# Bringing Branch B's inverse rms to the channel rows: a DRAM scratch row instead of TensorE transposes

## The chip, the core and the metric

The kernel runs on one core of a Trainium2 chip. The time is device microseconds of one execution; before the change the median of three runs is 1976.4 us (1971.2 to 1978.23). A core has a matrix engine, TensorE (PE; its weight loads are shown apart as PEld), a vector engine (DVE), an activation engine (ACT), a general engine (POOL) and a queue engine (SP), on which every DMA of this kernel is issued. Each engine takes its instructions strictly in order. Matrix results land in PSUM, a small memory of banks of 128 × 512 fp32 values; everything else lies in SBUF, 128 partitions wide.

## The reference

One encoder layer is applied to two independent requests ("groups"), each 1024 tokens × 1024 channels, with shared weights. Cut to what matters:

```
h    = rms_norm(x, norm_g) * (1 + scale) + shift
qa, ka, va, za, qb, kb, vb, zb, ga, gb = split(h @ w_in)
oa   = gqa_attention(rope(rms(qa)), rope(rms(ka)), va) * silu(za)      # 8 heads of 64
ob   = softmax(q0 k0) @ v - lam * softmax(q1 k1) @ v                   # 4 heads of 128
ob   = rms_norm(ob, subln_g) * (1 - lam_init)                          # over a head's 128 channels
ob   = ob * silu(zb)
merged = sigmoid(ga) * (oa @ w_proj_a) + sigmoid(gb) * (ob @ w_proj_b)
y    = x + gate * (merged @ w_out)
```

The change concerns the fourth and fifth lines of Branch B: each token of each head is divided by the rms of its 128 values.

## The kernel before

All of it is fp32 made from pairs of a rounded high part and a low rest, so a product takes three matmuls; scores and the values of a head are kept with channels on the partitions and tokens along the row. The two groups run one after the other. A group has these parts:

- the input projection, woven with attention: `qa_gen`, `qkb_gen`, `vb_gen` (matmuls at L514), and the gate paths z, ga, gb by `z_gen` (matmuls at L703), whose results are put to DRAM at L712 as `zd`;
- `attention`: 32 units of Branch A, then 16 units of Branch B (four heads, each four pairs of query tiles). A unit has scores (L734, L735), a softmax (L736 to L738), `flip` (a vector transpose at L771 and four DMA copies at L776, `q<-p`), and the values (L796, L797 for A, L836 for B in `b_values`). Attention's instructions get a higher priority than the work woven around them;
- at the end of a Branch B unit the squares of the output are summed over channels by a matmul with a column of ones (L858), so that the sum has the tokens on the partitions, and copied to `ssB` (L860), [128 tokens, head, 8 tiles]. After a head's last unit POOL turns the 8 columns into inverse rms values (L863 to L866);
- `gated_gen`: for each half of the tokens (`hf`) and each block of 128 channels e (0 to 3 are Branch A, 4 to 7 the heads of Branch B), the attention output `od` and gate `zd` are loaded, the gate gets its SiLU (L931), both are multiplied, and the row is multiplied by its per-token factor `rb`, which must now lie along the row and be the same on every partition (L946). Then the high part (L947, ACT) and low part (L948, DVE) are written for the projection;
- `merge_gen` for Branch A and then Branch B: 16 products of 12 matmuls each (L976), each multiplied by a sigmoid gate that is loaded at L966; the gate's sigmoid is at L967, the product with A's result at L987, with B's at L982;
- `out_gen`: the output projection (L1005).

For Branch A the factor comes through DRAM: the 64 rows of inverse sums are transposed once, stored as `rA` (L918), and each tile loads its row to 64 partitions at a time into a tile of the tag `tab` (L935), two buffers deep. The same two buffers hold the tables cosA and sinA earlier in a group. For Branch B the factor comes by TensorE: each column of 128 tokens is broadcast to 128 columns and transposed with the identity, four times for the 512 tokens of a tile (L941), into a PSUM bank, and L946 reads it there. There are 2 groups × 4 heads × 2 halves = 16 such tiles, so 64 transposes.

PSUM: three banks of the tag `f`, and two double banks `s` for scores. `gbank()` gives an `f` bank, or, where no attention runs (`alone`), the first half of an `s` bank on two of five calls.

What sets the order: `weave` interleaves the generators by weights written out by hand. Heads 0 and 1 (i = 2) of `gated_gen` are woven into the last stretch of attention; heads 2 and 3 (i = 3) into the last six merges of Branch A (half 0) and the start of Branch B's merges (half 1). From that order a planner that simulates the engines with its own costs makes the order of each engine, SP's included, at build time.

Of the kernel before, what the change touches and what calls it, by code (L numbers as in the profile page):

```python
# [12 lines left out]
F32 = mybir.dt.float32  # L13
# [7 lines left out]
P = 128  # L21
# [3 lines left out]
NTT = T // P  # L25
# [65 lines left out]
def kernel(ctx: ExitStack, tc: tile.TileContext, t: dict):  # L91
    nc = tc.nc
# [11 lines left out]
    dpool = ent(tc.tile_pool(name="dpool", bufs=1, space=DRAM))  # L104
# [6 lines left out]
    def nm(s):  # L111
        uid[0] += 1
        return f"{s}_{uid[0]}"

    def sbank():
        return ps_s.tile([P, 1024], F32, tag="s", name=nm("s"))
# [4 lines left out]
    def gbank():  # L121
        turn[0] += 1
        if alone[0] and turn[0] % 5 in (0, 2):
            return sbank()[:, :512]
        return fbank()

    def fbank():
        return ps_f.tile([P, 512], F32, tag="f", name=nm("f"))
# [24 lines left out]
    def mtile(tag, shape, dt=F32, bufs=None):  # L153
        return mpool.tile(shape, dt, tag=tag, name=nm(tag), bufs=bufs)

    def rtile():
        return mtile("row", [P, 512], bufs=3)

    dma = nc.sync.dma_start
# [8 lines left out]
    ident = const.tile([P, P], F32, name="ident")  # L168
# [551 lines left out]
    def query_order(x):  # L720

        return x.rearrange("p (t i b) -> p i t b", t=2, i=4)

    def piece_order(x):
        return x.rearrange("p (i t b) -> p i t b", t=2, i=4)
# [94 lines left out]
    def b_values(u):  # L820
        acc = ps_a.tile([P, 512], F32, tag="a", name=nm("a"))[:, :256]
        ready = []
        def pv(cc, th, tl):
            for c in range(2):
                k = cc * 2 + c
                for s, rt in ((0, th), (0, tl), (1, th)):
                    nc.tensor.matmul(
                        acc, u["v"][:, k, s, :], rt[:, c, :],
                        start=(k == 0 and s == 0 and rt is th), stop=(k == 7 and s == 1),
                    )  # L830

        if WHOLE[u["h"] // 2]:
            pT = u["pT"].bitcast(F32).rearrange("p (q c b) -> p c q b", q=8, c=8)
            yield 1
            for k in range(NCH):
                nc.tensor.matmul(acc, u["v"][:, k], pT[:, k], start=(k == 0), stop=(k == 7))  # L836
                if k % 2:
                    yield 1
        else:
            for piece in pT_pieces(u):  # L840
                ready.append(piece)
                if len(ready) > PV_LAG:
                    pv(*ready.pop(0))
                yield 1
            while len(ready) > 1:
                pv(*ready.pop(0))
                yield 1
            pv(*ready.pop())
        sq = mtile("at", [P, 256], bufs=1)
        o = mtile("oo", [P, 256])  # L850
        nc.scalar.activation(query_order(sq), piece_order(acc), AF.Square)
        nc.vector.tensor_copy(query_order(o), piece_order(acc))
        pr = u["pr"]
        dma(u["od"][pr // 2][:, (pr % 2) * 256 : (pr % 2 + 1) * 256], o)
        yield 1
        ps = fbank()
        for i in range(2):
            nc.tensor.matmul(ps[:, i : i + 1], sq[:, i * P : (i + 1) * P], ones_c, start=True, stop=True)  # L858
        ss = u["ss"][:, u["h"]]
        nc.vector.tensor_copy(ss[:, pr * 2 : pr * 2 + 2], ps[:, 0:2])  # L860
        if pr == 3:
            su = u["su"]
            nc.gpsimd.tensor_tensor(out=su, in0=su, in1=su, op=ALU.mult)  # L863
            nc.gpsimd.tensor_scalar(out=su, in0=su, scalar1=2.0 * HD * EPS, scalar2=1.0, op0=ALU.mult, op1=ALU.mult)
            nc.gpsimd.tensor_tensor(out=ss, in0=ss, in1=su, op=ALU.add)
            nc.gpsimd.tensor_tensor(out=ss, in0=ss, in1=nhalf[:, :NTT], op=ALU.pow)  # L866
        yield 1

    def attention(units):
# [39 lines left out]
    def gated_gen(st, i, hf, oT):  # L909

        if i == 0 and hf == 0:
            su = st["suA"].rearrange("p j n -> p (j n)")
            nc.vector.reciprocal(su, su)
            ps = fbank()[:64, :P]
            nc.tensor.transpose(ps, su, ident)
            row = rtile()[:64, :P]
            nc.scalar.activation(row, ps, AF.Copy)
            dma(st["rA"], row)  # L918
        rA = st["rA"].rearrange("(j h n) p -> j h (n p)", j=8, h=2)
        u = utile().rearrange("p (c s n) -> p c s n", c=2, s=2)  # L920
        oT.append(u)
        if i == 3:
            room = pair()
            os_, zs_ = ([room[:, (2 * a + c) * 512 : (2 * a + c + 1) * 512] for c in range(2)] for a in range(2))
        for c in range(2):
            e = 2 * i + c
            o, z = (os_[c], zs_[c]) if i == 3 else (rtile(), rtile())
            dma(o, st["od"][e][hf])
            dma(z, st["zd"][(e, hf)])
            if i >= SILU:  # L930
                nc.scalar.activation(z, z, AF.Silu)  # L931
            if e < 4:
                rb = mtile("tab", [P, 512])
                for a in range(2):
                    dma(rb[a * 64 : a * 64 + 64], rA[2 * e + a, hf].partition_broadcast(64))  # L935
                nc.vector.tensor_tensor(out=o, in0=o, in1=z, op=ALU.mult)
            else:
                rb = gbank()
                for k in range(4):
                    r = st["ssB"][:, e - 4, hf * 4 + k : hf * 4 + k + 1]  # L940
                    nc.tensor.transpose(rb[:, k * P : (k + 1) * P], r.to_broadcast([P, P]), ident)  # L941
                nc.vector.scalar_tensor_tensor(
                    out=o, in0=o, scalar=subg, in1=z,
                    op0=ALU.mult, op1=ALU.mult,
                )
            nc.vector.tensor_tensor(out=o, in0=rb, in1=o, op=ALU.mult)  # L946
            nc.scalar.activation(u[:, c, 0, :], o, AF.Copy)  # L947
            nc.vector.tensor_tensor(  # L948
                out=u[:, c, 1, :], in0=o, in1=u[:, c, 0, :].bitcast(F32), op=ALU.subtract
            )  # L950
            yield 1
# [80 lines left out]
    def new_state(g):  # L1032
        st = {"ht": {}, "qa": {}, "qkb": {}, "vb": {}, "zd": {}, "gad": {}, "gbd": {}, "md": {}}
        for name, n in (("suA", 8), ("suB", 4), ("ssB", 4)):
            st[name] = const.tile([P, n, NTT], F32, tag=name, name=nm(name), bufs=2 if name == "ssB" else 1)
        st["rsA"] = const.tile([P, 2, NTT, 4], F32, tag="rsA", name=nm("rsA"), bufs=1)
        st["qkb"]["rs"] = const.tile([P, 4, NTT, 4], F32, tag="rsB", name=nm("rsB"), bufs=1)
        st["rA"] = dpool.tile([64, P], F32, name=nm("rA"))
        st["od"] = [
            [dpool.tile([P, 512], F32, name=nm("od")) for _ in range(2)] for _ in range(8)  # L1040
        ]
        return st

    def units_of(st):

        def a_unit(half, i, pr):
            j = half * 4 + i
            kv = j // 4
            return {
                "q": [st["qa"][half][i % 2][:, i // 2]], "k": [st["ka"][:, kv]],  # L1050
                "v": (lambda k: st["va"][:, k, kv, :]),
                "pr": pr, "j": j, "od": st["od"][j // 2], "su": st["suA"][:, j],
                "rs": lambda qt, m: st["rsA"][:, half, qt, i : i + 1],
            }

        def b_unit(h, pr):
            qk = st["qkb"][h]
            return {
                "q": [qk[m][:, 0] for m in range(2)], "k": [qk[m][:, 1] for m in range(2)],
                "v": st["vb"][h], "pr": pr, "h": h,  # L1060
                "rs": lambda qt, m: st["qkb"]["rs"][:, h, qt, m : m + 1],
                "od": st["od"][4 + h], "ss": st["ssB"], "su": st["suB"][:, h],
            }

        def there(kind, n, pr):
            return made.get(id(st[kind].get(n)), 0) > 2 * pr + 1

        units = []
        for half in range(2):
            units += [  # L1070
                (half, lambda a=(half, i, pr): a_unit(*a), lambda a=("qa", half, pr): there(*a))
                for i in (0, 2, 1, 3) for pr in range(4)
            ]
        for h in range(4):
            units += [
                (2 + h, lambda a=(h, pr): b_unit(*a), lambda a=("qkb", h, pr): there(*a)) for pr in range(4)
            ]
        return units
# [23 lines left out]
    for g in range(2):  # L1102
        st = states[g]
# [108 lines left out]
```

## Time and profile before

| | |
|---|---|
| median of 3 runs | 1976.4 us (1971.2 to 1978.23) |
| span of the profiled execution | 1971.9 us |
| granted TensorE clock, mean | 0.990 |
| DMA, share of 16 engines | 50.1% |

The profile is of one execution, and its span (first to last instruction) is the time that it shows for that execution; no other time of it is given. An engine's line gives busy time, its share of the span and the count of instructions. A row of a group gives the line, engine, operation, output and inputs, the count, then busy time and mean length in ns, then the idle time before and what ended it. Rows of one line's instructions give the shortest, median and longest duration in ns, and the first and last start in us. A row of the chain of waits is start, length and piece of work. A row of waits gives who waited for whom: us in total, times, the longest. A row of stretches gives the stretch, its length, then busy time with count for PE, PEld, DVE, ACT and POOL, the granted clock, the DMA share and GB/s. A row of DMA issues gives the size and the median us from issue to landing. In the timeline, rows are start, length, engine, line and operation, with idle time before it in brackets.

### The profile page before, as it was taken

What the parts mean: (1) busy time and instruction counts of PE and PEld (TensorE: products, weight loads), DVE (VectorE), ACT (ScalarE), POOL (GpSimd) and SP (SyncE); (2) the same over time, 40 slices, a digit from 0 to 9 for tenths busy, and PEclk for the clock granted to TensorE, in tenths of its full rate; (3) what the DMA queues carried; (4) which work ended last, traced back from release to release, by engine and by line L of the source; (5) the groups of instructions that cost most, each with busy time, mean ns of one, the idle gap of its engine ahead of it and who ended that gap; (6) DMA issues with size and microseconds to landing.
All of it is one profiled execution on the core that took longest, in us unless ns stands there. A gap on an engine that the chain in (4) does not pass through costs nothing. (4 is left out here: it accounts for less than half of the span.)

```text
span 1971.9 us, 30870 instructions
## 1 busy us (share of the span) xinstructions
PE 1901.8 (96%) x10466; PEld 1619.1 (82%) x10466; DVE 1353.0 (69%) x2165; ACT 1012.0 (51%) x1920; POOL 680.9 (35%) x958
## 2 busy tenths in 40 slices
PE   8999999999989999999999999999999999998999
PEld 3888888888878985778889788888888889776887
DVE  4658876786888577757465598768878766776641
ACT  4447655565655353464323576556666444447410
POOL 2363511442446251322235344114444426322210
PEclk9899999999999999999999999999999999999999
DMA  9125545556454345865641355555555334478431
GB/s 315 33 89 149 144 139 149 158 156 174 127 144 111 89 117 173 272 234 179 222 151 44 115 144 167 148 149 157 156 152 161 98 102 119 120 222 267 166 102 75
DMA packets 271614, 295.26 MB, mean 150 GB/s; under 512 B 37856, under 2 KB 220256, under 8 KB 271456
## 3 DMA queue, kind: packets, MB, share of 16 engines
q1 hardware_dynamic: 271456, 293.28, 50.1%
q8 instruction: 84, 1.38, 0.3%
q14 instruction: 74, 0.61, 0.1%
HBM read 133.72 MB, written 42.01 MB: 89 GB/s over the span
## 5 line engine op out<-in xcount | busy, mean ns | idle before, releaser
L703 PE MATMUL f<-u,w 128*128 128x512 f32 x2184 | 561.3, 395 | 3.0 <-ACT w L179 1.3
L514 PE MATMUL f<-w,u 128*128 128x256 f32 x3456 | 489.6, 286 | 5.2 <-ACT ev L709 2.7
L514 PEld LDWEIGHTS f<-w,u 128*128 128x128 f32 x3456 | 460.7, 192 | 26.8 <-ACT ev L709 3.7
L703 PEld LDWEIGHTS f<-u,w 128*128 128x128 f32 x2184 | 396.8, 189 | 78.1 <-ACT w L179 1.8
L181 POOL TENSOR_TENSOR w<-st,w 128x512 fp32r<-128x512 f32 x166 | 227.8, 1391 | 463.2 <-ACT w L179 412.9
L736 DVE TENSOR_REDUCE m<-s 128x1 f32<-128x1024 f32 x256 | 310.2, 1217 | 55.1 <-PE s L735 52.0
L771 DVE STREAM_TRANSPOSE p<-p 128x1024 f32<-128x1024 f32 x192 | 238.0, 1241 | 112.8 <-ACT p L738 110.2
L785 DVE TENSOR_TENSOR q<-q,hi 128x512 fp32r<-128x512 f32 x256 | 193.9, 774 | 47.9 <-ACT hi L784 46.4
L738 ACT ACTIVATE p<-s,m,rsB 128x1024 f32<-128x1024 f32 x128 | 154.0, 1204 | 135.0 <-DVE m L737 103.3
L738 ACT ACTIVATE p<-s,m,rsA 128x1024 f32<-128x1024 f32 x128 | 153.8, 1202 | 128.1 <-DMA q<-p 95.8
L735 PE MATMUL s<-u,sw 128*128 128x512 f32 x512 | 205.0, 401 | 0.0
L784 ACT ACTIVATE hi<-q 128x512 fp32r<-128x512 f32 x256 | 153.2, 624 | 78.2 <-DMA q<-p 50.2
L179 ACT ACTIVATE w<-st 128x512 fp32r<-128x512 f32 x196 | 114.2, 626 | 101.9 <-DMA st<-in_w_in_dram 46.6
L976 PE MATMUL f<-u,w 128*128 128x512 f32 x552 | 136.4, 400 | 11.3 <-ACT ev L709 4.1
L796 PE MATMUL a<-hi,u 128*128 128x256 f32 x512 | 132.0, 284 | 4.8 <-DVE oo L813 3.1
L976 PEld LDWEIGHTS f<-u,w 128*128 128x128 f32 x552 | 104.8, 192 | 35.3 <-DVE u L987 4.6
L836 PE MATMUL a<-q,u 128*128 128x256 f32 x512 | 125.9, 385 | 5.6 <-DMA q<-p 1.9
L797 PE MATMUL a<-q,u 128*128 128x256 f32 x512 | 129.8, 287 | 0.5 <-DVE q L785 0.4
L734 PE MATMUL s<-u 128*128 128x512 f32 x256 | 109.5, 428 | 7.9 <-ACT p L738 4.0
L734 PE MATMUL s<-u,u 128*128 128x512 f32 x256 | 103.3, 404 | 13.8 <-ACT p L738 9.0
L836 PEld LDWEIGHTS a<-q,u 128*128 128x128 f32 x512 | 95.9, 193 | 21.6 <-issue 2.9
L735 PEld LDWEIGHTS s<-u,sw 128*128 128x128 f32 x512 | 97.4, 190 | 15.5
(186 smaller groups left out, 2639.1 us busy)
## 6 DMA issues: line engine op xcount, KB each, us to landing
q<-p SPq DMA_DIRECT2D x768, 128.0 KB, 2.6
st<-in_w_in_dram SPq DMA_DIRECT2D x132, 256.0 KB, 3.0
zd<-ev SPq DMA_DIRECT2D x96, 256.0 KB, 2.2
sw<-u SPq DMA_DIRECT2D x256, 64.0 KB, 2.0
p<-zd SPq DMA_DIRECT2D x64, 256.0 KB, 3.8
u<-in_w_ada_dram SPq DMA_DIRECT2D x8, 1024.0 KB, 10.4
st<-in_w_in_dram SPq DMA_DIRECT2D x64, 128.0 KB, 2.7
st<-in_w_out_dram SPq DMA_DIRECT2D x32, 256.0 KB, 3.2
```

Of the source, the lines that this page charges most:

```text
L181: e.tensor_tensor(out=wl, in0=st, in1=wh.bitcast(F32), op=ALU.subtract)
L514: nc.tensor.matmul(ps, lt[c][:, sl], w[:, c, wi, :], start=(k == 0), stop=(k == 23))
L703: nc.tensor.matmul(ps, w[:, c, wi, e * P : (e + 1) * P], rt[c], start=(k == 0), stop=(k == 23),)
L734: nc.tensor.matmul(s[:, sl], q, k[:, sl], start=True, stop=False)
L735: nc.tensor.matmul(s[:, sl], sw, k[:, sl], start=False, stop=True)
L736: nc.vector.tensor_reduce(out=m, in_=s, axis=AX.X, op=ALU.max, negate=True)
L738: nc.scalar.activation(pt.rearrange("p (j c a) -> p j c a", j=4, c=8), s.rearrange("p (c a j) -> p j c a", c=8, j=4), AF.Exp, scale=rs, bi ...
L771: nc.vector.transpose(pt, pt)
L784: nc.scalar.activation(th, tl.bitcast(F32), AF.Copy)
L785: nc.vector.tensor_tensor(out=tl, in0=tl.bitcast(F32), in1=th.bitcast(F32), op=ALU.subtract)
L836: nc.tensor.matmul(acc, u["v"][:, k], pT[:, k], start=(k == 0), stop=(k == 7))
L976: nc.tensor.matmul(ps, w[:, c, wi, d * P : (d + 1) * P], o[:, oi, :], start=(k == 0), stop=(k == 11))
```

## The change

After POOL's power at L866, the head's [128 tokens, 8 tiles] of inverse rms values are stored, transposed, to a DRAM scratch tile `rB` of [8, 128]; there is one such tile for each head and group, so 8 stores. In `gated_gen` a Branch B tile then loads its 512 values (four rows of the scratch, which lie in one piece) to all 128 partitions by one DMA, into a tile of the tag `tab`, and L946 reads this tile. The 64 transposes and the 16 `gbank()` calls are gone.

```diff
             nc.gpsimd.tensor_tensor(out=ss, in0=ss, in1=nhalf[:, :NTT], op=ALU.pow)
+            dma(u["rB"].rearrange("n p -> p n"), ss)
         yield 1
...
+            rb = mtile("tab", [P, 512])
             if e < 4:
-                rb = mtile("tab", [P, 512])
                 for a in range(2):
                     dma(rb[a * 64 : a * 64 + 64], rA[2 * e + a, hf].partition_broadcast(64))
                 nc.vector.tensor_tensor(out=o, in0=o, in1=z, op=ALU.mult)
             else:
-                rb = gbank()
-                for k in range(4):
-                    r = st["ssB"][:, e - 4, hf * 4 + k : hf * 4 + k + 1]
-                    nc.tensor.transpose(rb[:, k * P : (k + 1) * P], r.to_broadcast([P, P]), ident)
+                r = st["rB"][e - 4][hf * 4 : hf * 4 + 4].rearrange("n p -> (n p)")
+                dma(rb, r.partition_broadcast(P))
                 nc.vector.scalar_tensor_tensor(
...
+        st["rB"] = [dpool.tile([NTT, P], F32, name=nm("rB")) for _ in range(4)]
...
-                "od": st["od"][4 + h], "ss": st["ssB"], "su": st["suB"][:, h],
+                "od": st["od"][4 + h], "ss": st["ssB"], "rB": st["rB"][h], "su": st["suB"][:, h],
```

## The prediction

> **What bounds the kernel now.** I read the page first: TensorE (PE) is busy for 96% of the span, so the first question about any edit is whether it lies where PE never pauses.
>
> ```profile
> span 1971.9 us, 30870 instructions
> PE 1901.8 (96%) x10466; PEld 1619.1 (82%) x10466; DVE 1353.0 (69%) x2165; ACT 1012.0 (51%) x1920; POOL 680.9 (35%) x958
> ```
>
> PE idles for 1971.9 − 1901.8 = 70 us in all. Next I cut the span into stretches around the places where the removed transposes stand (the first columns are the stretch, its length, then PE's busy time):
>
> ```profile
> 637.00:831.00 194.00, 188.40 (x1008) 152.06 (x1006) 135.03 (x214) 84.48 (x163) 65.45 (x105) 1.00 0.54 159
> 841.20:889.50 48.30, 48.28 (x225) 40.19 (x226) 24.34 (x39) 29.76 (x38) 11.98 (x10) 0.96 0.68 230
> 889.50:990.00 100.50, 100.50 (x450) 83.31 (x449) 63.91 (x87) 39.89 (x66) 24.25 (x18) 1.00 0.59 201
> 990.00:1113.00 123.00, 121.86 (x732) 108.09 (x730) 65.53 (x155) 47.20 (x115) 56.74 (x73) 1.00 0.30 97
> 1764.00:1816.10 52.10, 44.27 (x193) 34.34 (x191) 37.22 (x55) 38.78 (x51) 9.53 (x10) 0.97 0.78 255
> 1816.10:1881.00 64.90, 64.86 (x293) 53.61 (x294) 44.98 (x66) 27.89 (x41) 15.57 (x12) 1.00 0.48 160
> ```
>
> In group 0 all eight bursts of transposes lie in 841 to 889.5, where PE is full, and it stays full to 1113. In group 1 five bursts lie in 1764 to 1816, where PE idles 7.8 us, and three after 1816, where it is full to the end. The chain of waits in order of time confirms this for group 1 (start, length, piece):
>
> ```profile
> 1792.27 0.70 DVE row L946
> ...
> 1793.11 4.51 PE f L976 x12
> ...
> 1819.66 8.38 PE f L976 x36
> 1828.04 0.44 PE s L941 x4
> 1828.48 2.75 PE s L976 x12
> 1831.23 5.44 PE f L976 x24
> 1836.67 0.44 PE s L941 x4
> 1837.11 0.44 PE f L941 x4
> ```
>
> From 1819.66 on the chain is PE alone, and three bursts of L941 are pieces of it, 0.44 us each.
>
> **Term 1, the 64 transposes go.** Their price has to be read with care. By groups of instructions and by order of time:
>
> ```profile
> L941 PE MATMUL f<-ident,ssB 128*128 128x128 f32 x48 | 7.2, 276 | 0.3 <-DVE ssB L860 0.3
> L941 PE MATMUL s<-ident,ssB 128*128 128x128 f32 x16 | 2.6, 272 | 0.0
> ```
>
> ```profile
> 888.75 1.03 PE L941 MATMUL f<-ident,ssB 128*128 128x128 f32 x8
> 889.54 4.58 PE L976 MATMUL s<-u,w 128*128 128x512 f32 x19
> ```
>
> One is shown as 272 ns long, which would make 64 × 0.272 = 17.4 us. But matmuls overlap: eight of them move the next matmul by only 889.54 − 888.75 = 0.79 us, 0.10 us each, and the chain gives 0.44/4 = 0.11. I take 0.10 to 0.11: in group 0 32 × 0.10 = 3.2 us, on the path; in group 1 three bursts × 0.44 = 1.3 us on the path, and the other five (2.2 us) at nothing, because PE waits beside them for other work; were that wait gone they would count too. Term 1: −4.5; ends −6.7 and 0 (something else late in their place, term 5).
>
> The Trainium skill, "TensorE: Matmul & The Clock Gate", Part 4: PE-mode transpose, gives about 275 ns for a transpose in a kernel's context; this trace agrees on the duration (272 ns) and not on the room it takes in a full stream (0.10 us); by the page's figure the gain would be an estimated 17.6 us. Nothing below uses that figure.
>
> **Term 2, sixteen PSUM banks are no longer taken.** The broadcast rows rb held a bank from the transposes to the multiply at L946. Waits of PE in 1764 to 1840 (sum, times, longest):
>
> ```profile
> PE f L976 <- DVE u L987: 3.9, 3, 2.6
> PE f L976 <- DVE row L946: 3.0, 2, 2.5
> ```
>
> The second row is a merge matmul that needs the bank which L946 still reads. After one of these gaps twelve matmuls took 4.51 us (at 1793.11) against 2.75 us (at 1828.48), 1.76 us more, in a stretch whose granted clock is 0.97: a gap costs more than its length. If both rows and that slow start went, 3.0 + 3.9 + 1.76 = 8.7 us. But the next limit is the same chain of sigmoid and SiLU inputs that feeds L987, so I take −1; ends −8.7 and 0. L946 itself costs the same from SBUF as from PSUM, so DVE gets nothing:
>
> ```profile
> L946 DVE TENSOR_TENSOR row<-tab,row x16: 643/683/1620, 782.4 to 1782.4; 128x512 f32<-128x512 f32 x16
> L946 DVE TENSOR_TENSOR row<-f,row x8: 674/682/692, 847.9 to 1818.9; 128x512 f32<-128x512 f32 x8
> ```
>
> **Term 3, eight stores of ss to scratch.** Each writes 128 × 8 values transposed, so 1024 pieces of 4 bytes, issued by SP, which holds everything behind it (the flips' q<-p copies, weights, gate loads) until POOL's power at L866 is done. No such store is in the trace. The nearest rows: the branch A scratch (rA, rows of 512 bytes), and the cosB and sinB tables, also 1024 pieces; for the waiting, the L854 store, also fed by b_values (in all, times, longest).
>
> ```profile
> tab<-rA SPq DMA_DIRECT2D x32, 128.0 KB, 3.7
> ...
> cosB<-in_cosB_dram SPq DMA_DIRECT2D x2, 64.0 KB, 4.7
> ...
> rA<-row SPq DMA_DIRECT2D x2, 32.0 KB, 2.8
> ```
>
> ```profile
> L413 SPq DMA_DIRECT2D sinB<-in_sinB_dram x2: 582/1810/3037, 40.2 to 43.2; - x2
> ```
>
> ```profile
> SPq L854 <- DVE oo L852: 20.0, 13, 2.6
> ```
>
> Issue: 0.6 us free, 3.04 us when earlier pieces fill the queue (sinB). Wait: 20.0/32 stores = 0.6 us. So each store holds SP about 1.2 us. Six of the eight (heads 0 to 2) stand in attention stretches; PE there is busy 188.4 of 194, so part is absorbed by slack, part makes a q<-p copy late and stalls PE. I take half: 6 × 0.6 = +3.6; ends 0 and 6 × 3.04 = +18.2. A gain is excluded, since nothing is taken from SP there.
>
> **Term 4, sixteen broadcast loads.** Each is one issue on SP, as at L935:
>
> ```profile
> L935 SPq DMA_DIRECT2D tab<-rA x32: 444/501/598, 773.8 to 1769.7; - x32
> ```
>
> 16 × 0.50 = 8 us of SP. In group 0 it is hidden by the full PE. In group 1 about half of them fall in 1764 to 1816, which is set by loads and activations; I take two that push a gate load: +1.0; ends 0 and +4 (8 × 0.50). The tile comes from the tab buffers, two deep, so each load also waits for an L946 two tiles back, and group 1's cosA table, which uses the same buffers, moves behind group 0's last tile, near 890. Its first user is at 1028, so that is free:
>
> ```profile
> L546 DVE TENSOR_TENSOR rc<-row,tab x5: 281/292/424, 1028.3 to 1057.6; 128x128 f32<-128x128 f32 x4, 128x256 f32<-128x256 f32 x1
> ```
>
> **Term 5, the last head's round trip.** Heads 0 to 2 have their factor long before it is wanted. Head 3 has not: its power is the last thing attention does, and branch B's first merge wants it for its last three matmuls. POOL, the queue, and the multiply-to-split tail (L946 to L948):
>
> ```profile
> 873.51 1.65 POOL L866 TENSOR_TENSOR ssB<-ssB,nhalf 128x8 f32<-128x8 f32 x1
> ...
> 1824.53 1.65 POOL L866 TENSOR_TENSOR ssB<-ssB,nhalf 128x8 f32<-128x8 f32 x1
> ```
>
> ```profile
> 872.05 6.11 SPq L221 DMA_DIRECT2D st<-in_w_proj_b_dram  x3
> ```
>
> ```profile
> 881.60 0.68 DVE L946 TENSOR_TENSOR q<-f,q 128x512 f32<-128x512 f32 x1
> 885.02 0.69 DVE L948 TENSOR_TENSOR u<-q,u 128x512 fp32r<-128x512 f32 x1 [2.74 <-ACT u L947]
> ...
> 1828.69 0.68 DVE L946 TENSOR_TENSOR q<-s,q 128x512 f32<-128x512 f32 x1
> ...
> 1831.02 0.69 DVE L948 TENSOR_TENSOR u<-q,u 128x512 fp32r<-128x512 f32 x1 [1.65 <-ACT u L947]
> ```
>
> The tail is 885.71 − 881.60 = 4.1 us in group 0, 1831.71 − 1828.69 = 3.0 us in group 1. Store to landing is 2.8 (rA) to 4.7 us (cosB), the load 3.7. Group 0: the power ends at 875.2, but SP may sit in the weight loads until 878.2; ready at 875.2 + 2.8 + 3.7 + 3.0 = 884.7 at best, 878.2 + 4.7 + 3.7 + 4.1 = 890.7 at worst. Wanted: the first B merge starts at 889.5, its tenth matmul 9/12 × 2.75 = 2.1 us later, and term 1 brings that forward by 3.1, so 888.5. Group 1: power 1826.2, ready 1835.7 to 1838.7, wanted at 1837.5 + 2.1 − 1.3 = 1838.3. In both the middle is in time by about a microsecond. I take 0; ends 0 and (2.2 + 0.4) + 1.8 for one slow restart = +4.4.
>
> **Sum.** −4.5 − 1.0 + 3.6 + 1.0 + 0 = −0.9 us. The profiled execution's span is 1971.9 and the median of the runs 1976.4, 4.5 above it; no row shows what lies around the span, so I carry the difference over: 1976.4 − 0.9, about 1975. A change of under 0.5% (9.9 us, so 1966.5 to 1986.3) is about what a measurement of this kernel can't tell from none.
>
> **Rivals.**
> *Banks set the tail.* If the waits on L946 and L987 both come from too few banks, −4.5 − 8.7 gives 1963. For it: the wait on L946 is on the chain. Against: the other row is the longer and L987 waits for loaded gates.
> *The whole busy time comes off*, −17.4: 1959. The spacing in the trace speaks against it.
> *The 4-byte stores hold SP.* Every attention store costs 3.04 us on the path: −4.5 − 1 + 18.2 + 1 = +13.7, 1990; it turns the sign of the verdict from 2.4 us a store on. For it: the sinB row, one queue for everything, the flips' copies behind it. Against: sinB's 3.04 came behind three tables of 1024 pieces. The Trainium skill, "DMA: Bandwidth & Descriptors", Specifications, says transfers below 512 bytes become read-modify-write; no row here shows a 4-byte write, and this rule would push towards this case.
> *The round trip is late.* A store of 10 us makes group 0 ready at 875.2 + 10 + 3.7 + 3.5 = 892.4 (3.9 late), group 1 at 1843.4 (5.1 late), with two slow restarts +12.5 in all: 1988. It decides from a store of about 8 us.
> *The planner reorders.* The build plans the order with its own costs, so other work may swap places after the first store. A sixth more PE idling (70/6) gives +11.7: 1987. No row can show it.
>
> **How the numbers follow.** Forecast 0.55 (within 0.5%); banks 0.12 and whole busy time 0.02 (faster); stores hold SP 0.16, round trip late 0.07, planner 0.08 (slower). So faster 0.14, same 0.55, slower 0.31. The likeliest case's own range is 1967 to 1986; the range given is 1964 to 1990, which leaves out about half of the gains and a third of the losses, 0.17.
>
> **What would show it.** Right: no L941; the stretch after group 1's last attention step full on PE and 1 to 2 us shorter; the stretch 841 to 890 shorter by 3; an SP issue of the new store near 0.6 us. Wrong: PE waiting for the multiply of head 3 at the start of branch B's merge (term 5); a store issue of several us, or q<-p waits grown in attention (term 3); waits of L976 on the banks gone with more than 5 us (term 2); a different order of PE before the first store.

## The result, and the profile after

The changed kernel takes 2006.05 us (2002.56 to 2011.19, four runs), the kernel before, measured beside it, 1973.95 us (1971.2 to 1978.23). The ratio is 1.0166 (1.0145 to 1.0187): **32.1 us slower**, far outside the half per cent that counted as no change. The forecast was 1975 and its range ended at 1990.

The profiled execution has a span of 2009.4 us and a time of 2011.19, so 1.8 us lie around the span. (Line numbers: the new store is L867, the new load L940; lines from old L941 to L1005 are one lower, so the head's multiply L946 is now L945, a merge matmul L976 is L975. In kernels where the transposes stay, they are one higher.)

Where on the way the time is lost shows in the lines' rows of PE: count, shortest, median and longest duration in ns, first and last start. First the merge matmuls and the output projection of the kernel before, then of the kernel after:

```profile
L976 PE MATMUL f<-u,w x552: 387/389/632, 831.5 to 1878.0; 128*128 128x512 f32 x184
...
L1005 PE MATMUL f<-u,w x456: 388/389/389, 932.7 to 1967.8; 128*128 128x512 f32 x152
```

```profile
L975 PE MATMUL f<-u,w x552: 387/389/796, 842.8 to 1918.2; 128*128 128x512 f32 x184
...
L1004 PE MATMUL f<-u,w x456: 388/389/389, 953.2 to 1999.8; 128*128 128x512 f32 x152
```

The first merge matmul of group 0 starts 11.3 us later, the first of the output projection 20.5 us later; the spans differ by 37.5 us. The rest goes in the same places of group 1. Up to the first store the two programs run the same instructions in the same order, and this execution is already some 4 us behind (power of the first head at 641.40 against 637.22), so that much of the 37.5 is the difference between two executions.

The DMA issues of the kernel after (size, median us from issue to landing), and the new store by itself (duration on SP in ns, then issue to landing, shortest, median and longest):

```profile
tab<-rA SPq DMA_DIRECT2D x32, 128.0 KB, 3.9
tab<-rB SPq DMA_DIRECT2D x16, 256.0 KB, 5.7
rB<-ssB SPq DMA_DIRECT2D x8, 4.0 KB, 10.4
rA<-row SPq DMA_DIRECT2D x2, 32.0 KB, 2.7
```

```profile
L867 SPq DMA_DIRECT2D rB<-ssB x8: 372/398/595, 643.7 to 1855.9; - x8
...
DMA to landing us min/median/max: 7.6/10.4/11.7
```

This is the row that the forecast lacked: 4 KB take 10.4 us to land, while the 32 KB of `rA` take 2.7. On SP the same store takes only 0.40 us; whoever looks at the queue's instruction alone sees nothing of it.

What PE waited for, what DVE's head multiply waited for, and what SP's load waited for (us in all, times, longest), kernel after:

```profile
PE s L734 <- ACT p L738: 26.0, 14, 5.7
PE f L975 <- DVE u L986: 13.7, 3, 9.0
PE f L975 <- ACT u L946: 9.1, 1, 9.1
```

```profile
DVE q L945 <- DMA tab<-rB: 31.0, 7, 12.8
```

```profile
SPq L940 <- DMA rB<-ssB: 17.9, 2, 9.4
```

The scores' row in the kernel before:

```profile
PE s L734 <- ACT p L738: 13.0, 15, 1.6
```

Two things stand there. One is the head multiply waiting for its factor, with two gaps of about 9 us on PE. The other is the softmax being late: before, scores waited 13.0 us in 15 places for `p`, at most 1.6 at a time; now 26.0, up to 5.7. The experiments take them apart.

The chain of waits after group 1's last power, in order of time (start, length, piece), shows the first of the two whole:

```profile
1854.20 1.66 POOL ssB L866
...
1855.88 10.11 DMA rB<-ssB
...
1866.00 0.32 SPq L940
...
1866.37 6.24 DMA tab<-rB
...
1872.71 0.06 DVE q L945
...
1875.87 4.59 PE s L975 x12
...
1885.93 2.72 PE s L975 x12
```

The value is there at 1855.86 and the multiply has it at 1872.7: 10.1 us of store, 6.2 of load. PE stands 9 us, and the next twelve matmuls take 4.59 us where a full stream takes 2.72. In group 0 the same (PE in order of time, idle before it and its cause in brackets; in this view twelve matmuls of a full stream show 2.88):

```profile
887.59 2.88 PE L975 MATMUL f<-u,w 128*128 128x512 f32 x12
899.46 4.89 PE L975 MATMUL f<-u,w 128*128 128x512 f32 x12 [8.98 <-DVE u L986]
```

The name in the brackets is the instruction that came last before the gap ended (L986). It stood on DVE behind the multiply L945, which had waited 11.18 us for the load (DVE in order of time), and group 1's gap on PE is as long (PE again):

```profile
897.51 1.29 DVE L945 TENSOR_TENSOR q<-tab,q 128x512 f32<-128x512 f32 x2 [11.18 <-DMA tab<-rB]
898.72 0.68 DVE L986 TENSOR_TENSOR u<-f,p 128x512 f32<-128x512 f32 x1
```

```profile
1873.22 0.79 PE L975 MATMUL f<-u,w 128*128 128x512 f32 x1 [9.12 <-ACT u L946]
```

### The profile page after: what moved, and what is told of

The parts are those of the page before. It is cut to its first block, busy times and chain, and to the rows that moved or that the text cites. A ratio compares the mean times of both kernels' runs of the same rounds, so it can differ in the third digit from the quotient of the medians.

```text
span 2009.4 us, 30794 instructions
## 1 busy us (share of the span) xinstructions
PE 1907.2 (95%) x10402; PEld 1623.9 (81%) x10402; DVE 1359.1 (68%) x2165; ACT 1009.6 (50%) x1919; POOL 683.0 (34%) x958
## 5 line engine op out<-in xcount | busy, mean ns | idle before, releaser
L738 ACT ACTIVATE p<-s,m,rsB 128x1024 f32<-128x1024 f32 x128 | 153.9, 1203 | 143.0 <-DVE m L737 104.9
L738 ACT ACTIVATE p<-s,m,rsA 128x1024 f32<-128x1024 f32 x128 | 153.8, 1202 | 130.5 <-DMA q<-p 90.8
L975 PE MATMUL f<-u,w 128*128 128x512 f32 x552 | 140.1, 408 | 28.2 <-DVE u L986 13.7
L975 PEld LDWEIGHTS f<-u,w 128*128 128x128 f32 x552 | 108.2, 197 | 54.6 <-DVE u L986 15.0
L734 PE MATMUL s<-u 128*128 128x512 f32 x256 | 109.8, 429 | 17.2 <-ACT p L738 16.9
L734 PE MATMUL s<-u,u 128*128 128x512 f32 x256 | 105.0, 410 | 13.1 <-ACT p L738 9.0
L569 ACT ACTIVATE u<-f 64x256 fp32r<-64x256 f32 (+1 forms) x200 | 72.3, 363 | 80.1 <-DVE u L570 57.9
## 6 DMA issues: line engine op xcount, KB each, us to landing
u<-in_w_ada_dram SPq DMA_DIRECT2D x8, 1024.0 KB, 10.4
```

Of the source, the lines that this page charges most:

```text
L734: nc.tensor.matmul(s[:, sl], q, k[:, sl], start=True, stop=False)
L738: nc.scalar.activation(pt.rearrange("p (j c a) -> p j c a", j=4, c=8), s.rearrange("p (c a j) -> p j c a", c=8, j=4), AF.Exp, scale=rs, bi ...
L975: nc.tensor.matmul(ps, w[:, c, wi, d * P : (d + 1) * P], o[:, oi, :], start=(k == 0), stop=(k == 11))
```

## The experiments

Three explanations stood against each other. The last head's round trip is late. Or the store is dear in itself, and what it delays is other work, whether anyone reads it or not. Or it is something else: SP held by issues and loads, or a new order of the planner. Each ratio is against the kernel before, measured beside it (medians 1973.7 to 1974.2).

**Stores alone.** The kernel before, with the eight stores added and read by nobody:

```diff
             nc.gpsimd.tensor_tensor(out=ss, in0=ss, in1=nhalf[:, :NTT], op=ALU.pow)
+            dma(u["rB"].rearrange("n p -> p n"), ss)
```

> The kernel before, with the 8 stores to scratch added and nobody reading them; the 64 transposes stay. Theory 1: nobody waits for the stores, so the time is that of before within 0.5%, 1969 to 1980. Theory 3: the queue is held and its rings are filled with 8 x 1024 pieces, at least 10 us slower, over 1984. Theory 2: a planner's order that differs after the first store, slower by an unknown amount up to 1995.

Measured: 2000.72 us, ratio 1.0126 (1.0105 to 1.0147), +26.5 of the +32.1 us. In the two traces 10420 of PE's 10466 matmuls come in the same order (by line and output), and up to 820 us no two are exchanged. So no reader is needed for most of the loss, and hardly any reordering; a run further down, with the very same order, takes that out too. How it acts is seen after the third store. SP, ACT and PE of this kernel in order of time:

```profile
801.04 0.38 SPq L867 DMA_DIRECT2D rB<-ssB  x1
...
802.94 1.09 SPq L936 DMA_DIRECT2D tab<-rA  x2
...
805.74 0.43 SPq L221 DMA_DIRECT2D st<-in_w_proj_a_dram  x1
809.14 5.32 SPq L776 DMA_DIRECT2D q<-p  x4
```

```profile
809.93 0.63 ACT L948 ACTIVATE u<-row 128x512 fp32r<-128x512 f32 x1 [8.21 <-DVE row L947]
815.11 0.63 ACT L222 ACTIVATE w<-st 128x512 fp32r<-128x512 f32 x1 [4.55 <-DMA st<-in_w_proj_a_dram]
815.65 0.37 ACT L851 ACTIVATE at<-a 128x256 f32<-128x256 f32 x1
815.94 1.20 ACT L738 ACTIVATE p<-s,m,rsB 128x1024 f32<-128x1024 f32 x1
```

```profile
817.29 0.80 PE L734 MATMUL s<-u 128*128 128x512 f32 x1 [5.92 <-ACT p L738]
```

and the same weight rounding on ACT, the same place on PE, and the four copies on SP, in the kernel before:

```profile
806.36 0.63 ACT L222 ACTIVATE w<-st 128x512 fp32r<-128x512 f32 x1 [0.92 <-DMA st<-in_w_proj_a_dram]
```

```profile
810.23 0.50 PE L734 MATMUL s<-u 128*128 128x512 f32 x1 [1.07 <-ACT p L738]
```

```profile
803.71 2.56 SPq L776 DMA_DIRECT2D q<-p  x4
```

The rounding L222 starts at 815.11, 9.4 us after the load of its weight was issued at 805.74, behind the store. ACT had already waited 8.21 us before L948 (5.34 in the kernel before); it now waits 4.55 us more for the weight. The softmax (L738) comes right behind on ACT, and PE waits 5.92 us for it. In the kernel before the weight is 0.92 us late and PE idles 1.07 us there. The four copies stretch over 5.32 us on SP instead of 2.56, though each one's own issue is 0.6 us. So it is the transfers issued after the store that are late, not the store's own issue.

This trace has no landing times of the store, but the kernel after has the same chain with them: the store issued at 803.53 landed at 815.08, the weight load issued behind it at 808.23 landed at 817.75, and the second of the four copies went out at 815.10. PE's gap there is 5.67 us.

The stretch 638 to 650, around the first store, tells why. Columns: stretch, length, busy time of PE, PEld, DVE, ACT, POOL, granted clock, DMA share, GB/s. The kernel before, then stores alone:

```profile
638.00:650.00 12.00, 12.00 (x89) 11.44 (x88) 8.85 (x13) 4.28 (x9) 3.55 (x7) 1.00 0.49 132
```

```profile
638.00:650.00 12.00, 12.00 (x92) 11.54 (x90) 8.26 (x12) 4.46 (x10) 2.79 (x7) 1.00 0.73 119
```

The DMA engines are busy for 73% of the time instead of 49% and move no more, 119 GB/s and 132: 0.24 of the 12 us, some 3 us of all 16 engines, comes on top with one store of 4 KB. In this stretch PE stays full (12.00 of 12.00), so the first head's store costs nothing here; the third one falls where there is no such reserve.

**Stores alone, 128 pieces of 32 bytes.** The scratch is laid out so that each partition's eight values are one piece:

```diff
-            dma(u["rB"].rearrange("n p -> p n"), ss)
+            dma(u["rB"].rearrange("n p -> (n p)").rearrange("(p n) -> p n", n=NTT), ss)
```

> As the kernel with the stores alone (2000.7 us; transposes kept, nobody reads the scratch), but each store writes its 4 KB as 128 pieces of 32 bytes, one per partition, in place of 1024 pieces of 4 bytes. Queue, place, bytes and the power it waits for are the same, and TensorE's order is that of before up to the last tenth. Theory A, the 1024 pieces fill the 16 DMA rings for about 10 us and every copy behind them is late: the 26 us go, 1970 to 1979. Theory B, the queue's wait for POOL's power is what costs: still 1995 to 2003.

Measured: 1978.22, ratio 1.002 (1.0007 to 1.0033). The same bytes from the same instruction at the same place: +4.1 us instead of +26.5. So the form of the write decides, not the fact that there is a store. (The order on PE differs a little from that of the first run: 10251 of 10466 matmuls stand at the same place.)

**Stores alone, 512 pieces of 4 bytes.** Half the columns, otherwise as the first:

```diff
-            dma(u["rB"].rearrange("n p -> p n"), ss)
+            dma(u["rB"].rearrange("n p -> p n")[:, :4], ss[:, :4])
```

> The stores alone again (transposes kept, nobody reads the scratch), each with only four of its eight columns: 512 pieces of 4 bytes, half the bytes. With 1024 pieces 2000.7 was measured, with 128 pieces 1978.2. Theory A, the time goes with the number of pieces in the rings: a landing of about 6 us instead of 10, and 1984 to 1992. If it were a matter of any 4-byte store at all: near 2000. If only of long backlogs: near 1976.

Measured: 1996.19, ratio 1.0117 (1.0101 to 1.0134). Half of the pieces keep 22.5 of the 26.5 us, above the 1984 to 1992 expected of a price by the piece. The cost isn't one price for each piece, as I had held by then.

**Stores alone, the same 1024 pieces farther apart.** A scratch tile of [128, 8, 2] gives each partition 64 bytes of its own, with its eight values 8 bytes apart; one of [128, 8, 16] puts every value 64 bytes from the next:

```diff
-            dma(u["rB"].rearrange("n p -> p n"), ss)
+            dma(u["rB"][:, :, 0], ss)
```

> The stores alone (transposes kept, nobody reads the scratch), 1024 pieces of 4 bytes, but each partition's eight pieces lie in 64 bytes of their own (8 bytes apart), so that no two partitions write into the same 64 bytes. If the 4-byte piece itself costs: 1996 to 2004, as with the transposed row (2000.7). If it is neighbours written by different engines: near the 128 pieces, 1975 to 1983.

> The same with every piece 64 bytes from the next, so that no two pieces share 64 bytes at all. If the 4-byte piece itself costs: 1996 to 2004. If pieces that share 64 bytes wait for each other: 1975 to 1983, also where the run with eight pieces in 64 bytes stays slow.

Measured: 1985.79, ratio 1.0059 (1.0036 to 1.0081), and 1979.81, ratio 1.0027 (1.0008 to 1.0046). The first lies between its two expectations, the second where pieces that wait for each other in 64 bytes would put it. The store's issue and landing in four of these kernels, in the order 512 pieces, own 64 bytes, 64 bytes apart, 128 pieces of 32 bytes (one fence each; last figure: median us to landing):

```profile
rB<-ssB SPq DMA_DIRECT2D x8, 2.0 KB, 9.3
```

```profile
rB<-ssB SPq DMA_DIRECT2D x8, 4.0 KB, 7.0
```

```profile
rB<-ssB SPq DMA_DIRECT2D x8, 4.0 KB, 4.1
```

```profile
rB<-ssB SPq DMA_DIRECT2D x8, 4.0 KB, 2.2
```

Put beside the times, the landing sorts them all (the trace of the first run has no landing):

| the store | pieces | values in the same 64 bytes | landing, us | time over before, us |
|---|---|---|---|---|
| as in the change | 1024 of 4 B | 16, of 16 partitions | 10.4 (in the kernel after) | +26.5 |
| half the columns | 512 of 4 B | 16, of 16 partitions | 9.3 | +22.5 |
| 64 B for each partition | 1024 of 4 B | 8, of one partition | 7.0 | +12.1 |
| 64 B between values | 1024 of 4 B | 1 | 4.1 | +6.2 |
| one piece a partition | 128 of 32 B | 16, of 2 partitions | 2.2 | +4.1 |

With the same 1024 pieces the time goes from +26.5 to +6.2 when the values no longer lie close together. In the traces of the stores alone with 1024 pieces side by side, with 512, with 64 bytes for each partition and with 64 bytes between values, every engine does the same work in the same order, and SP makes the same issues in the same order. Only the scratch's layout (and for 512 the count) differs, so the planner's order has no part in these differences. So small pieces written into the same few bytes are the larger part of the price. Their number is the smaller part, if it counts at all: 1024 and 512 pieces, and the last two rows of the table, have intervals that overlap.

The 12 us from the third store's issue on show what becomes of the transfers (columns as above; first side by side, then 64 bytes apart):

```profile
801.04:813.04 12.00, 10.34 (x48) 8.39 (x47) 6.95 (x5) 1.32 (x3) 3.75 (x3) 1.00 0.94 120
```

```profile
796.67:808.67 12.00, 10.66 (x49) 8.68 (x49) 9.40 (x13) 3.79 (x8) 5.52 (x5) 1.00 0.85 229
```

At a busy share that is no lower the engines move 120 GB/s instead of 229. Set matmul against matmul, the first of these two executions falls 25.1 us behind the second. Some 6 us of this arise at PE's gap behind the third store, 5.5 behind the fourth (a gap of 4.03 us and slow matmuls after it), 7 behind group 1's third; the rest is spread out.

Whether 64 bytes is the bound, and whether it matters that neighbours come from different partitions, these runs can't say: both changed together, and no other spacing was tried. Nor do they show whether the writes queue up in the memory or in the DMA engines.

**The reader without the stores.** The change with no store; the loads read rows of `rA` instead, so Branch B's factors are wrong ones:

```diff
-            dma(u["rB"].rearrange("n p -> p n"), ss)
...
-                dma(rb, r.partition_broadcast(P))
+                dma(rb, rA[e - 4, hf].partition_broadcast(P))
```

> The change without its stores; the 16 broadcast loads read rows of branch A's scratch, which has long landed, so branch B is multiplied by wrong factors. It leaves the loads and the gain of the removed transposes. With no loads at all 1971.0 was measured. Theory A: the loads cost 0 to 5 us, 1971 to 1976, and what the change has beyond that is the store and the wait for it. If the loads themselves were the cost: 1980 or more.

**Neither transposes nor scratch.** The gate itself takes the factor's place, so Branch B's headwise rms is left out:

```diff
-                rb = gbank()
-                for k in range(4):
-                    ...
+            rb = mtile("tab", [P, 512]) if e < 4 else z
```

> Neither transposes nor scratch: branch B's rows are multiplied by the gate a second time in place of the inverse rms, so that part of the computation (headwise rms of branch B) is left out. It gives the most that taking away the transposes and the banks can bring: theory 1 expects 1974 - 4.5 to 1974 - 13, 1961 to 1970. Theory 2, the planner's order changes anyway: 1974 or more, up to 1995.

Measured: 1973.85, ratio 0.9988 (0.9971 to 1.0005), and 1970.99, ratio 0.9984 (0.9971 to 0.9997). All that the change can gain is 3.2 us; with the sixteen loads put in it is 0.3. These two intervals overlap, so the loads' price, about 2.9 us, is known only roughly; but the loads by themselves are not the 32 us. The second run lies just above what I expected of it for the transposes and banks (1961 to 1970).

**The last head.** Heads 0 to 2 through DRAM and head 3 by transposes, and the reverse:

```diff
+            if u["h"] < 3:
                 dma(u["rB"].rearrange("n p -> p n"), ss)
...
+                if e == 7:
+                    ...
+                        nc.tensor.transpose(rb[:, k * P : (k + 1) * P], r.to_broadcast([P, P]), ident)
```

> Heads 0 to 2 go through DRAM as in the change; head 3 keeps the 16 transposes and has no store. Theory 1: both stalls of TensorE at head 3 (9.0 and 9.1 us, with a slow restart each) go, so 2006 - 18 to 2006 - 22, 1984 to 1988. Theory 2: 2000 to 2008. Theory 3: 6 of 8 stores remain, 2000 to 2004.

> Only head 3 of each group goes through DRAM as in the change (2 stores of 1024 pieces, 4 loads); heads 0 to 2 keep their transposes. With heads 0 to 2 through DRAM and head 3 by transposes it was 1994.9, 20.7 over before. If the parts add up, head 3 has the rest of the 32 us: 1983 to 1988. If head 3's round trip of 16 us is hidden by the merges: 1972 to 1978.

Measured: 1994.86, ratio 1.0103 (1.0081 to 1.0126), and 1997.21, ratio 1.0122 (1.0102 to 1.0142). Both miss what was expected of them. Taking head 3's trip and its two stores away gives back 11.2 us of the 32.1; head 3 alone costs 23.5 us, and 20.7 + 23.5 is more than the whole. For head 3 alone the trace accounts for the size: PE stands once in each group,

```profile
896.55 11.15 PE L981 MATMUL f<-u,w 128*128 128x512 f32 x36 [8.87 <-DVE u L992]
...
1856.77 5.17 PE L981 MATMUL f<-u,w 128*128 128x512 f32 x12 [10.53 <-DVE u L992]
```

19.4 us in all, and the matmuls behind the gaps start some 5 us slower than a full stream. In the kernel after the two gaps and slow starts come to 22 us in the same way. So the late round trip is there in full; what is open is why taking it away gives back only half of that. The parts may cover each other, and the run without head 3 also has another order on PE; neither was taken apart.

**The loads on another queue.** The sixteen loads issued by POOL, so that SP doesn't stand at L940:

```diff
-                dma(rb, r.partition_broadcast(P))
+                nc.gpsimd.dma_start(rb, r.partition_broadcast(P))
```

> The change, with the 16 broadcast loads issued by POOL; the stores stay on SP with their 1024 pieces. SP no longer stands still until head 3's store has landed (17.9 us in all in the change), but the rings are as full. If standing still costs: 1988 to 1996. Theory A: the rings and the round trip stay, 2000 to 2008.

Measured: 2016.47, ratio 1.0213 (1.0185 to 1.0241), slower still, and above both expectations. The waiting is moved, not removed (POOL, us in all, times, longest):

```profile
POOL tab L940 <- DMA rB<-ssB: 20.0, 2, 10.1
```

POOL's own work now stands behind the store twice, so this run alone doesn't price SP's standing still. But with the stores alone SP never stands for a store to land, and 26.5 us are lost: it is not the main cost.

**Fewer and longer pieces, with the reader.** Three versions of the change. In the first, TensorE turns the head's eight columns at once, and eight rows of 512 bytes are stored:

```diff
-            dma(u["rB"].rearrange("n p -> p n"), ss)
+            ps = fbank()[:NTT, :P]
+            nc.tensor.transpose(ps, ss, ident)
+            row = rtile()[:NTT, :P]
+            nc.scalar.activation(row, ps, AF.Copy)
+            dma(u["rB"], row)
```

> The scratch row stays, but each head's 8 columns are turned by one transpose on TensorE and stored as 8 rows of 512 bytes (8 transposes instead of 64). Theory 1, the round trip of head 3 is late (the store of 4-byte pieces took 10.4 us, the branch A row store 2.7): each group gets back 10.4 - 2.7 = 7.7 us, so about 2006 - 15 = 1991 us. Theory 2, the planner's new order costs the time: no gain, 2000 to 2008. Theory 3, the stores hold the queue in attention: the gain is larger than 15 us, below 1985.

In the second, the 128 pieces of 32 bytes of above, so that the factors are permuted among the tokens:

```diff
-            dma(u["rB"].rearrange("n p -> p n"), ss)
+            dma(u["rB"].rearrange("n p -> (n p)").rearrange("(p n) -> p n", n=NTT), ss)
```

> The change with the store in 128 pieces of 32 bytes; the scratch then holds the factors in another order, so the tokens get each other's inverse rms: that part of the computation is changed, the work is not. Theory A: 26 of the 32 us go, and the round trip of head 3 is shorter by 7, so 1974 to 1984. Theory B: 2000 to 2008. The planner's order as the cause (TensorE's order here is nearly the change's): 1995 or more.

In the third, DVE turns blocks of 32 × 32 and four stores put 8 pieces of 128 bytes each:

```diff
-            nc.gpsimd.tensor_tensor(out=ss, in0=ss, in1=nhalf[:, :NTT], op=ALU.pow)
-            dma(u["rB"].rearrange("n p -> p n"), ss)
+            w = tiny.tile([P, 32], F32, tag="w32", name=nm("w32"), bufs=2)
+            nc.vector.memset(w, 0.0)
+            nc.gpsimd.tensor_tensor(out=w[:, :NTT], in0=ss, in1=nhalf[:, :NTT], op=ALU.pow)
+            nc.vector.transpose(w, w)
+            for q in range(4):
+                dma(u["rB"][:, q * 32 : q * 32 + 32], w[q * 32 : q * 32 + NTT])
```

> The change with the right factors and few pieces: VectorE turns the head's columns in blocks of 32 (columns 8 to 31 are zero), and four stores put 8 pieces of 128 bytes each. Theory A: like the store in 128 pieces (1978.2), with three more issues on SP a head, 1974 to 1984. If a round trip over DRAM costs by itself at head 3, whatever its pieces: 1985 or more.

Measured: 1982.47, ratio 1.0038 (1.0026 to 1.005); 1978.19, ratio 1.0017 (0.9991 to 1.0043); 1974.97, ratio 1.0007 (0.9995 to 1.002). All three take back most of the loss, the third all of it. The first gained more than a shorter round trip was expected to give (1991), which fits stores that cost time in attention too. With the third version the way through DRAM costs nothing measurable and gains nothing. DVE's wait for the factor shrinks with it, from the 31.0 us in 7 places of the kernel after to this in the third version:

```profile
who waited for it (us, times):
  DVE q L949: 8.5, 3
```

Last, the third version with head 3 left to the transposes, to see whether the round trip still costs something there:

```diff
+            if u["h"] == 3:
+                nc.gpsimd.tensor_tensor(out=ss, in0=ss, in1=nhalf[:, :NTT], op=ALU.pow)
+            else:
                 w = tiny.tile([P, 32], F32, tag="w32", name=nm("w32"), bufs=2)
...
+            rb = gbank() if e == 7 else mtile("tab", [P, 512])
```

> As the block turn for heads 0 to 2, but head 3 keeps its 16 transposes, so that nothing waits for a round trip. Theory A: between no factor at all (1971.0) and the kernel before, 1968 to 1976, and a few us under the block turn alone. If the changed order of the last stretches costs as much as the round trip: equal to the block turn within 3 us.

Measured: 1981.99, ratio 1.004 (1.0025 to 1.0056), slower than with head 3 in DRAM, against what was expected. With a store that lands fast the round trip is no loss; what makes this version 7 us slower was not found. A changed plan may do this, which no run here shows by itself.

No version with the right factors was measurably faster than the kernel before, and the run without any factor puts what could be had this way at 0.16% (0.03 to 0.29).

## Why the prediction was wrong

**Failed: what the new store does once it is issued.** Term 5 took its landing from "the nearest rows", 2.8 us (`rA`) to 4.7 us (cosB). Term 3 left the landing out: it priced only SP's time and put what the store does to the transfers behind it at nothing, without a reason. The landing measured 10.4. The `rA` rows are pieces of 512 bytes, and cosB's 1024 pieces are read from DRAM and not written to it; neither is the same thing as 4-byte pieces written side by side. What the sum took for the nearest rows differed in the one property that mattered. The Trainium skill, "DMA: Bandwidth & Descriptors", Specifications, states that transfers below 512 bytes become read-modify-write. The runs agree in direction (10.4 us for 4-byte pieces, 2.2 for 32-byte ones), but 32-byte pieces are below that size as well and cost 4.1 us where the 4-byte pieces cost 26.5; the rule alone doesn't separate the two.

**Term 3, +3.6 forecast, +26.5 measured, with the wrong mechanism.** The term looked for the harm on SP: an issue of 0.6 to 3.04 us, and a wait for POOL's power. The issue measured 0.40 us and SP's waits for POOL before it 3.5 us for all eight, so a store holds SP some 0.8 us where 1.2 was taken: what the term priced was not too small. The rival of 1990, in which each store itself holds SP for 3.04 us, was wrong by its own mark as well, though it was right that later issues are slowed (the four copies, 5.32 us for 2.56). The harm is in the transfers behind the store. In the kernel after, ACT waits 24.1 us in 7 places for the weights of the projections (L222), before 3.8 in 3; the longest of these loads takes 13.5 us to land for 6.1, and the median of the gate loads `p<-zd` is 4.9 for 3.8. So the upper end, +18.2, was not a bound at all: it bounded the issue and left the transfers behind it out. The forecast's own mark, grown waits on `q<-p`, was the wrong place too: PE's wait for `q<-p` at L734 was 6.1 us before and is 2.2 now; it is the wait for the softmax that doubled, at its longest place through ACT's weight rounding.

**Term 5, 0 forecast, 11.2 to 23.5 measured.** The mechanism was named rightly and the size was missed. The rival of 1988 had it: with a store of 10 us it worked out to 12.5 us, two late round trips with two slow restarts, deciding from a store of 8 us. The store took 10.1 us in group 1, the trip 16.8, the two gaps 8.98 and 9.12, with restarts of 4.89 us for 2.88 and 4.59 for 2.72, 22 us in all. The run with head 3 on transposes gives 11.2 us back (two of the eight stores go with it), and head 3 alone costs 23.5. It got a chance of 0.07 because I trusted the landing of other rows.

**The two together** are the outcome that no rival held: both losses hang on the same number, so they came together. I had priced them apart, as if one excluded the other. The sum by measured parts: 26.5 for the stores, −0.3 for transposes replaced by loads, and 5.9 left for the readers that wait for the stores (by difference, not shown by itself), 32.1 in all. Since head 3 alone costs 23.5, these parts are not independent; the stores that nobody reads already cost time around head 3 (the gap of 4.03 us), and the late trip may cover part of that.

**Terms 1 and 2, −5.5 forecast, −3.2 measured together** (interval −5.7 to −0.6): right, within the interval. (One reading in term 2 was thin: of the two gaps behind its rows only the one before 1793.11 has a slow start; after the other, of 2.61 us before 1784.80, 24 matmuls took 5.78 us.) The 64 transposes, 17.4 us of shown duration, were worth no more than the room they took in the stream, and the rivals of 1963 and 1959 fall.

**Term 4, +1.0 forecast, about +2.9 measured**, inside its ends of 0 and +4, from two runs whose intervals overlap.

**The planner's order** was not the main cause: up to about 800 us the order on PE is the same in both kernels, and with the order of every engine kept, 1024 pieces cost +26.5 us side by side and +6.2 spread out. That other versions with changed orders differ by up to 7 us without a cause found says that its chance wasn't idle.

**The sum's base** had a small fault: of the 4.5 us carried from span to median, 1.8 lie around the span (2011.19 − 2009.4 in the kernel after, 2001.81 − 2000.0 with stores alone), the rest was the difference between executions.

## What to carry to other kernels

When a store turns a tile from partitions to rows, look at what it writes and not at how many bytes: here a DMA that scattered neighbouring 4-byte values delayed the transfers behind it, and its issue time on the queue showed none of this; the landing time and the DMA share against the GB/s did. Turn the tile on chip first, or lay the scratch out so that each partition writes one piece, if the reader can take that. And when two terms of a sum rest on the same unmeasured duration, they are one risk: price them with the high end together, and let the range reach that far.

## What the runs showed of the hardware

- A DRAM write of 4 KB took 10.4 us to land as 1024 neighbouring 4-byte pieces, 4.1 us with the pieces 64 bytes apart, 2.2 us as 128 pieces of 32 bytes. The rise with closeness at an equal number of pieces was unexpected; its mechanism is not shown.
- While such a store drains, the 16 DMA engines are no less busy and move about half as much: share 0.94 at 120 GB/s in the 12 us after the third store, 0.85 at 229 GB/s with the pieces 64 bytes apart. A transfer that has nothing to do with it is late: in the kernel after, the weight load issued 4.7 us after the store landed 9.5 us after its issue.
- After a gap of 9 us on PE the next twelve matmuls took 4.59 to 4.89 us, against 2.72 to 2.88 in a full stream. In the stretch that holds group 0's gap the granted clock was 0.91, in the stretch before it, where PE also idled 4.6 us, 0.90; in the same stretches of the kernel before it was 1.00 (columns as above; after, then before):

```profile
845.00:880.00 35.00, 30.43 (x126) 24.81 (x125) 19.82 (x32) 27.55 (x35) 9.63 (x10) 0.90 0.93 319
880.00:935.00 55.00, 46.02 (x195) 37.58 (x194) 29.28 (x39) 19.27 (x27) 11.38 (x8) 0.91 0.56 168
```

```profile
845.00:880.00 35.00, 35.00 (x169) 29.25 (x169) 18.98 (x30) 22.84 (x30) 8.75 (x8) 1.00 0.67 224
880.00:935.00 55.00, 55.00 (x251) 45.60 (x250) 40.15 (x60) 24.92 (x37) 9.33 (x7) 1.00 0.54 182
```
